# One early pair instead of three, and a different order of products, token transposes and gate rows in the feed-forward stage of a diffusion block

## Chip, cores and metric

The kernel runs on one core of a Trainium2 chip. The metric is the time of one execution on the device in microseconds; less is better. TensorE (PE) does the matmuls, ScalarE (ACT) and VectorE (DVE) move, split and combine tiles, and DMAs are issued from SyncE's queue (SP), from GpSimd's (POOL) and a few from ScalarE's.

## What is computed

One block of a bidirectional diffusion trunk on 640 tokens (128 of a prompt, 512 noisy ones) of width 1024: a mixer, then a feed-forward part with a gate. The change lies in the feed-forward part, whose reference is

```python
def block(x, cond, rows, states, w_ada, b_ada, norm1_w, norm2_w, mix_params, w_ff1, w_ff2):
    mod = (jax.nn.silu(cond) @ w_ada + b_ada)[:, None, :]
    sh1, sc1, g1, sh2, sc2, g2 = jnp.split(mod.astype(x.dtype), 6, axis=-1)
    ...
    x = x + g1 * y
    h = rmsnorm(x, norm2_w) * (1 + sc2) + sh2
    x = x + g2 * (jnp.square(jax.nn.relu(h @ w_ff1)) @ w_ff2)
    return x, new_states
```

w_ff1 is 1024 x 4096 and w_ff2 4096 x 1024. The conditioning differs between prompt and noisy tokens, so sc2, sh2 and g2 have two columns each.

## The kernel before

Every fp32 product is done as three matmuls of operands split into a high and a low part (`three`, lines 146 to 148: high by high, low by high, high by low). Splitting a tile is a copy on ScalarE (all ScalarE work has line 85) and a subtraction on DVE (line 107).

The 4096 hidden columns are 32 units of 128. Units 0 and 16 are done plainly (`plain`). Units p and p + 16 for p = 1 to 15 form a pair, whose 2 x 2 blocks are done with seven products instead of eight (`ff1`, `head`, `prod`): A11 and A12 into the PSUM tile pa, S2, S3 and A22 into pb, S1 and S4 into pc. The A's are halves of weights, the S's sums of them; the moving operands are input halves (hH, hL) and their sums T1 to T4 (tHL, and T4 in hH, hL). A product is 12 matmuls of 128x320 or 128x322. `ff2` then adds a pair's two hidden units into the output: ten sums of six matmuls 128x512, evacuated into y by ScalarE (the first pair's worth) or DVE (line 1278). One pair is 84 matmuls of the first kind and 60 of the second.

Weights come as follows. `direct` fetches A11 and A12 over POOL's queue: wh by a plain DMA (line 1147), its negative into wl by ScalarE, and the weight added into wl by an accumulating DMA (line 1149). `sums_of` loads s1 and s2 on SyncE's queue and forms S1 to S4 on DVE (lines 1029 to 1032). `second` loads the FF2 weights st2 on SyncE's queue and splits them. s1, s2 and st2 share a tag "st" with two buffers, s3 and gb a tag "sta" with two, wh and wl have three buffers each. SyncE's loads (`load`) keep the order of the program.

The order on each engine is made by a scheduler from the program and its priorities (`tc.high_priority()`), with `behind` for an order between two instructions of one engine that don't wait for each other by data. Every engine then runs its list in order.

`early(p)` does the products A11 and A12 ahead of the rest for p = 1, 2 and 3. Between these stand `to_tokens(0)` to `to_tokens(4)`: the 640 tokens of the residual are transposed back (40 transposes xT, line 1244), copied by ScalarE to xq and stored to DRAM as xtd over SyncE's queue (line 1246), to be added into y at pair 13. xq shares the tag "g" (four buffers) with the hidden units g. The vector cr, which `ada_dot` needs for the gate G2 at pairs 4 to 11, is read back from DRAM over SyncE's queue too (line 1236). At p = 12 `ada_bias` adds the bias and `g2_rows` turns G2's columns into rows: DVE spreads each of 16 columns over a 128x128 tile gb (line 1256), and PE transposes it (line 1257). m2 and m3 are the sums of products that DVE forms in sq (lines 1202 to 1205 and 1219); S3 goes into the same bank pb that m2 is read from, and A22 into the same bank that m3 is read from.

Of the kernel before, what the change touches and what calls it, by code (L numbers as in the profile page):

```python
# [19 lines left out]
P = 128  # L20
D = 1024
# [31 lines left out]
def hybrid_step(ctx: ExitStack, tc: tile.TileContext, I, O):  # L53
# [30 lines left out]
    def act(out, in_, func, **kw):  # L84
        ins = nc.scalar.activation(out, in_, func, **kw)  # L85
        if func in (AF.Exp, AF.Ln, AF.Silu, AF.Sigmoid):
            behind(ins.ins, tables["set"])
            tables["users"].append(ins.ins)
        return ins
# [925 lines left out]
    def comb(name):  # L1015
        return keep.tile([P, 4, HE], F32, tag="P%d" % (1 + int(name[1]) % 2), name=name)
# [2 lines left out]
        act(h, t_[:, :, 0:n], AF.Copy)  # L1019
        split_l(l, t_[:, :, 0:n], h)  # L1020

    def sums_of(p):
        s1 = stp.tile([P, 1024], F32, tag="st", name="s1")
        load(s1, I["wff1"][p])
        s2 = stp.tile([P, 1024], F32, tag="st", name="s2")
        load(s2, I["wff1"][p + 16])
        a, b = slice(0, 512), slice(512, 1024)
        s3 = stp.tile([P, 1024], F32, tag="sta", name="s3")[:, 0:512]
        tt(out=s3, in0=s1[:, a], in1=s2[:, a], op=ALU.subtract)  # L1029
        tt(out=s2[:, a], in0=s2[:, a], in1=s2[:, b], op=ALU.add)  # L1030
        tt(out=s1[:, a], in0=s2[:, a], in1=s1[:, a], op=ALU.subtract)
        tt(out=s1[:, b], in0=s1[:, b], in1=s1[:, a], op=ALU.subtract)
        return [("S1", s2[:, a]), ("S2", s1[:, a]), ("S3", s3)], (s2[:, b], s1[:, b])

    for b in range(4):
        def evac_o(acc):
            for f in range(2):
                k = 2 * b + f
                for hf, (lo, hi) in enumerate(SPANS):
                    for c, p0, p1 in pieces(lo, hi):  # L1040
                        stt(out=xr[:, k, p0:p1], in0=acc[f][hf][:, p0 - lo:p1 - lo], scalar=AB[:, G1, k, c:c + 1],
                            in1=xr[:, k, p0:p1], op0=ALU.mult, op1=ALU.add)
        proj_feat("wo", evac_o, part=o_part)
        for f in range(2):
            k = 2 * b + f
            square_add(sq2, xr[:, k, :], k, 0, T)
            for c, p0, p1 in CONDS:
                a2 = AB[:, SC2, k, c:c + 1]
                act(hH[:, k, p0:p1], xr[:, k, p0:p1], AF.Copy, scale=a2)
                stt(out=hL[:, k, p0:p1], in0=xr[:, k, p0:p1], scalar=a2, in1=hH[:, k, p0:p1].bitcast(F32),  # L1050
                    op0=ALU.mult, op1=ALU.subtract)
    r2 = ffp.tile([P, T], F32, name="r2")
    v2 = ffp.tile([P, T + 4], F32, name="v2")
    for lo, hi in SPANS:
# [9 lines left out]
    def unit(pool, name, src):  # L1064
        h = pool.tile([P, 512], F32R, tag=name + "h", name=name + "h")
        l = pool.tile([P, 512], F32R, tag=name + "l", name=name + "l")
        act(h, src, AF.Copy)
        split_l(l, src, h)
        return h, l

    def combined(p, out):
        with tc.high_priority():
            order_, rest = sums_of(p)
            for name, src in order_:
                out[name] = unit(sp, name, src)
        return rest

    def last_unit(out, src):
        with tc.high_priority():
            out["A22"] = unit(ff, "A22", src[0])  # L1080
            out["S4"] = unit(ff, "S4", src[1])

    splits = []

# [28 lines left out]
            act(hf[k // 4][:, :, T:T + 2], AB[:, SH2, k - 3:k + 1, :], AF.Copy)  # L1113
    zs = [plain(0)]
    ta, tb = comb("t1"), comb("t2")
    tt(out=ta[:, :, LO], in0=hf[0][:, :, HALF:T], in1=hf[0][:, :, LO], op=ALU.subtract)
    dve.tensor_copy(ta[:, :, HALF:HE], hf[0][:, :, T:T + 2])
    tt(out=tb, in0=hf[1][:, :, UP], in1=ta, op=ALU.subtract)
    store(tb, tH[:, 1], tL[:, 1])
    store(ta, tH[:, 0], tL[:, 0])  # L1120
    zs.append(plain(16))
    ta = comb("t3")
    tt(out=ta, in0=hf[1][:, :, UP], in1=hf[0][:, :, UP], op=ALU.subtract)
    store(ta, tH[:, 2], tL[:, 2])
# [49 lines left out]
            ins += three(ps[:, 0:n], A[0][:, s], A[1][:, s], B[0][:, k, :], B[1][:, k, :], start and k == 0, k == 3, skip=True)  # L1174
        return ins

    us = [v2[:, 0:HE], v2[:, HE:2 * HE], ff.tile([P, HE + 8], F32, name="u3")[:, 0:HE]]
    for t_ in us:
        dve.memset(t_[:, HALF:HE], 0.0)
    m2, m3 = sq2[:, 0:HE], sq2[:, HE:2 * HE]  # L1180
# [2 lines left out]
        return ff.tile([P, 2, T], F32R, tag="g", bufs=4, name="g")  # L1183

    def head(p, w):
        a = (xbank if p < 4 else bank)("pa")
        u = us[p % 3]
        prod(a, w["A11"], B11, True)
        act(u[:, LO], a[:, LO], AF.Copy)
        return a, u  # L1190

    def ff1(p, w, early=None):
        a, u = early or head(p, w)
        z0 = ffp.tile([P, T], F32, tag="u", bufs=2, name="z0")
        z1 = ffp.tile([P, T], F32, tag="u", bufs=2, name="z1")
        b = bank("pb")
        c = bank("pc")
        if early:
            tt(out=z0[:, LO], in0=a[:, LO], in1=r2[:, LO], op=ALU.mult)
        prod(b, w["S2"], T2, True)  # L1200
        prod(c, w["S1"], T1, True)
        tt(out=m2, in0=b[:, 0:HE], in1=u, op=ALU.add)
        prod(b, w["S3"], T3, False)
        tt(out=m3, in0=b[:, 0:HE], in1=u, op=ALU.add)
        tt(out=m3, in0=c[:, 0:HE], in1=m3, op=ALU.add)
        if not early:
            prod(a, w["A12"], B21, False)
            tt(out=z0[:, LO], in0=a[:, LO], in1=r2[:, LO], op=ALU.mult)
        ga, gb = g_tile(), g_tile()
        halves = ((HALF, T), (0, HALF)) if p == 15 else ((0, T),)  # L1210

        def z1_upper():
            tt(out=z1[:, HALF:T], in0=m3[:, LO], in1=r2[:, HALF:T], op=ALU.mult)

        if p == 15:
            z1_upper()
            finish(z1, m3[:, HALF:HE], gb, HALF)
        p3 = prod(c, w["S4"], B22, False)
        tt(out=m2, in0=c[:, 0:HE], in1=m2, op=ALU.add)
        tt(out=z0[:, HALF:T], in0=m2[:, LO], in1=r2[:, HALF:T], op=ALU.mult)  # L1220
        for lo, hi in halves:
            g0 = finish(z0, m2[:, HALF:HE], ga, lo, hi)
        p4 = prod(b, w["A22"], T4, False)
        if p == 15:
            behind(p4[0], p3[-1])
        if p < 15:
            z1_upper()
        tt(out=z1[:, LO], in0=b[:, LO], in1=u[:, LO], op=ALU.add)
        tt(out=z1[:, LO], in0=z1[:, LO], in1=r2[:, LO], op=ALU.mult)  # L1229
        g1 = finish(z1, m3[:, HALF:HE], gb, *halves[-1])  # L1230
        return g0, g1
# [1 line left out]
    cr = ff.tile([P, 2560], F32, tag="rows", name="cr")  # L1233
    junk = cr[:, 2048:2560].bitcast(BF16)
    cr = cr[:, 0:2048].rearrange("p (n k) -> p n k", k=D)
    nc.sync.dma_start(out=cr, in_=crd.unsqueeze(0).to_broadcast([P, 2, D]))
    xtd = dramp.tile([NT, P, D], F32, name="xtd")

    def to_tokens(c):
        t_ = ff.tile([P, 2, T], F32, tag="g", bufs=4, name="xq").rearrange("p i t -> p (i t)")  # L1240
        for q in range(2):
            pt = xbank("xT")
            for i in range(4):
                nc.tensor.transpose(pt[:, i * P:(i + 1) * P], xr[:, 4 * q + i, c * P:(c + 1) * P], ident)
            act(t_[:, 512 * q:512 * q + 512], pt, AF.Copy)
        nc.sync.dma_start(out=xtd[c], in_=t_[:, 0:D])

    def g2_rows():
        rows = ff.tile([P, 2, 1024], F32, tag="rows", name="g2r")
        for n in range(2):  # L1250
            for q in range(2):
                pt = xbank("g2")
                gb = stp.tile([P, 1024], F32, tag="sta", name="gb")
                for i in range(4):
                    s = slice(i * P, (i + 1) * P)
                    ts(out=gb[:, s], in0=ones, scalar1=AB[:, G2, 4 * q + i, n:n + 1], scalar2=None, op0=ALU.mult)
                    nc.tensor.transpose(pt[:, s], gb[:, s], ident)
                act(rows[:, n, 512 * q:512 * q + 512], pt, AF.Copy)
        return rows

# [41 lines left out]
            (nc.scalar if i else nc.sync).dma_start(out=O["out_y"][c, :, h], in_=y[:, c, h])  # L1302

    g = {0: tuple(finish(z, ub, g_tile()) for z, ub in zs)}
    heads, units = {}, {}

    def early(p):
        w = units.setdefault(p, {})
        w.update(direct(p))
        a, u = head(p, w)  # L1310
        prod(a, w["A12"], B21, False)
        heads[p] = (a, u)

    units[1] = {}
    last_unit(units[1], combined(1, units[1]))
    early(1)
    to_tokens(0)
    early(2)
    to_tokens(1)
    to_tokens(2)  # L1320
    early(3)
    to_tokens(3)
    to_tokens(4)
    y = ffp.tile([P, NT, D], F32, tag="X", name="y")
    for p in range(1, 16):
        w1 = units.get(p, {})
        if p > 1:
            last_unit(w1, combined(p, w1))
        if p > 3:
            w1.update(direct(p))  # L1330
        g[p] = ff1(p, w1, heads.get(p))
        if 4 <= p < 12:
            ada_dot(G2, p - 4, cr, junk, splits[-1])
        if p == 12:
            ada_bias(G2)
            rows = g2_rows()
        if p < 15:
            ff2(g.pop(p - 1), second(p - 1), acc_y(p - 1))
# [96 lines left out]
```

## Time and profile before

| | us |
|---|---|
| median of 3 runs | 840.62 |
| lowest, highest | 839.35, 843.19 |
| profiled execution | 841.95 |
| its span | 840.2 |
| PE busy in the span | 800.4 (95%) |
| DVE busy | 632.0 (75%) |
| ACT busy | 419.7 (50%) |
| POOL busy | 88.4 (11%) |

The span runs from the first to the last instruction of the profiled execution; 1.75 us of its time lie around it. Times in rows are counted from the span's start. The feed-forward stage begins at about 370 us. A matmul's row shows when it starts and how long it is in the pipeline; as matmuls overlap, what one costs is the distance between two starts. "xN" in a row joins N like instructions, and what stands in brackets is the idle time of the engine ahead of it and what ended that.

### The profile page before, as it was taken

Reading aid. Unit: us, or ns where it says so; the run is one execution under the profiler, and the core shown is the slowest. Engines: PE = TensorE matmul, PEld = TensorE weight load, DVE = VectorE, ACT = ScalarE, POOL = GpSimd, SP = SyncE. Lnnn points to the kernel's source line nnn. Section 1 sums busy time; section 2 is a strip of 40 time slices with the busy share of each in tenths; the row PEclk is TensorE's granted clock in tenths of the full one; section 3 lists DMA queues with packets and bytes.
Section 4 is the critical chain, followed back from the end, with each engine's and each line's share of the span. In section 5 each row is a group of like instructions: output and inputs, shape, how many; then the busy total and the mean of one; then the engine's idle time right before and its main releaser. Section 6 shows DMA issues by size and latency. Waiting matters only on the chain.

```text
span 840.2 us, 14783 instructions
## 1 busy us (share of the span) xinstructions
PE 800.4 (95%) x5842; PEld 705.6 (84%) x5842; DVE 632.0 (75%) x1188; ACT 419.7 (50%) x839; POOL 88.4 (11%) x123
## 2 busy tenths in 40 slices
PE   6999999999999999999899999999999998999995
PEld 2787688999988898998778898988899887788874
DVE  4668897868565569988467877787879878567858
ACT  5456458466554476655673444352345415324443
POOL 1121000030243003001000000000000000000200
PEclk9899999999999999999899999999999999899998
DMA  9926424141252073416642645545444535244923
GB/s 344 367 67 203 150 78 152 51 128 53 74 129 62 1 250 122 155 61 163 230 130 70 177 127 148 150 126 151 124 153 136 141 101 140 61 101 135 205 63 125
DMA packets 34197, 113.48 MB, mean 135 GB/s; under 512 B 4288, under 2 KB 5200, under 8 KB 33872
## 3 DMA queue, kind: packets, MB, share of 16 engines
q1 hardware_dynamic: 21888, 75.28, 26.5%
q0 software_dynamic: 8976, 30.50, 15.4%
q10 hardware_dynamic: 3264, 6.76, 2.3%
q8 instruction: 46, 0.75, 0.4%
q14 instruction: 23, 0.19, 0.1%
HBM read 106.66 MB, written 5.82 MB: 134 GB/s over the span
## 4 chain that ended last, share of the span: by engine, by line
PE 41%; issue 31%; DVE 12%; DMA 8%; ACT 5%; POOL 2%; DVEq 0%; SPq 0%; POOLq 0%; ACTq 0%
DMA st<-in_wff_dram 2%; PE ff L146 2%; PE ada L231 2%; PE ff L148 2%; PE ff L147 2%; PE pt L147 2%; PE pt L148 2%; PE pt L146 2%; DMA wh<-in_wff_dram 2%; PE pn L892 2%; PE pn L897 1%; DVE wl L107 1%; DMA xT<-in_xT_dram 1%; PE ob L148 1%; DMA s<-in_wff_dram 1%
## 5 line engine op out<-in xcount | busy, mean ns | idle before, releaser
L147 PE MATMUL ff<-wl,g 128*128 128x512 f32 x310 | 121.8, 396 | 0.0
L148 PE MATMUL ff<-wh,g 128*128 128x512 f32 x310 | 121.1, 396 | 0.0
L146 PE MATMUL ff<-wh,g 128*128 128x512 f32 x310 | 117.7, 399 | 3.3 <-ACT g L85 3.0
L1278 DVE TENSOR_TENSOR y<-ff,y 128x512 f32<-128x512 f32 x130 | 87.6, 688 | 10.7 <-PE ff L148 10.5
L107 DVE TENSOR_TENSOR wl<-st,wh 128x1024 fp32r<-128x1024 f32 x55 | 67.7, 1237 | 32.2 <-ACT wh L85 32.0
L85 ACT ACTIVATE wh<-st 128x1024 fp32r<-128x1024 f32 (+1 forms) x59 | 60.0, 1028 | 56.3 <-DMA st<-in_wff_dram 17.5
L146 PEld LDWEIGHTS ff<-wh,g 128*128 128x128 f32 x310 | 58.2, 189 | 16.3 <-ACT g L85 3.6
L148 PEld LDWEIGHTS ff<-wh,g 128*128 128x128 f32 x310 | 58.3, 188 | 13.4
L147 PEld LDWEIGHTS ff<-wl,g 128*128 128x128 f32 x310 | 58.5, 189 | 12.3
L147 PE MATMUL pt<-wl,hH 128*128 128x256 f32 x160 | 46.0, 288 | 0.2 <-DVE wl L107 0.2
L148 PE MATMUL pt<-wh,hL 128*128 128x256 f32 x160 | 45.6, 285 | 0.0
L146 PE MATMUL pt<-wh,hH 128*128 128x256 f32 x160 | 45.4, 286 | 0.0
L146 PE MATMUL pa<-hH,wh 128*128 128x320 f32 x120 | 38.8, 323 | 4.4 <-ACT u L85 3.7
L148 PE MATMUL pa<-hH,wl 128*128 128x320 f32 x120 | 38.8, 323 | 4.2 <-DMA wl<-in_wff_dram 4.2
L85 ACT ACTIVATE z<-z,sq 128x128 f32<-128x128 f32 (+3 forms) x62 | 31.4, 547 | 19.6 <-DVE z L1229 9.6
L85 ACT ACTIVATE S1h<-s 128x512 fp32r<-128x512 f32 x15 | 9.4, 628 | 62.7 <-DVE s L1030 45.9
L1147 POOL DMA_DIRECT2D wh<-in_wff_dram x15 | 8.4, 562 | 296.9 <-PE pa L148 197.7
L964 DVE SCALAR_TENSOR_TENSOR cr<-stg,cr 128x1024 f32<-128x1024 f32 (+1 forms) x32 | 39.1, 1220 | 0.1
L147 PE MATMUL pa<-hL,wh 128*128 128x320 f32 x120 | 38.3, 319 | 0.0
L1029 DVE TENSOR_TENSOR s<-s,s 128x512 f32<-128x512 f32 x15 | 10.4, 692 | 33.7 <-DMA s<-in_wff_dram 28.0
L107 DVE TENSOR_TENSOR g<-z,g 128x640 fp32r<-128x640 f32 (+1 forms) x34 | 25.9, 781 | 11.3 <-ACT g L85 11.3
L147 PEld LDWEIGHTS pt<-wl,hH 128*128 128x128 f32 x160 | 30.1, 188 | 3.3 <-issue 2.5
(459 smaller groups left out, 2414.4 us busy)
## 6 DMA issues: line engine op xcount, KB each, us to landing
st<-in_wff_dram SPq DMA_DIRECT2D x34, 512.0 KB, 3.7
sta<-in_ada_dram SPq DMA_DIRECT2D x32, 512.0 KB, 6.6
s<-in_wff_dram SPq DMA_DIRECT2D x30, 512.0 KB, 3.6
st<-in_win_dram SPq DMA_DIRECT2D x18, 512.0 KB, 3.7
stg<-in_adag_dram POOLq DMA_DIRECT2D x16, 512.0 KB, 3.8
wh<-in_wff_dram POOLq DMA_DIRECT2D x15, 512.0 KB, 3.9
wl<-in_wff_dram POOLq DMA_DIRECT2D x15, 512.0 KB, 5.5
st<-in_wout_dram SPq DMA_DIRECT2D x8, 512.0 KB, 3.9
```

The costliest lines, as they stand in the source:

```text
L85: ins = nc.scalar.activation(out, in_, func, **kw)
L107: return (eng or dve).tensor_tensor(out=dst, in0=src, in1=hi.bitcast(F32), op=ALU.subtract)
L146: first = mm(out, lhsT=ah, rhs=bh, start=start, stop=False, skip_group_check=skip)
L147: mm(out, lhsT=ah, rhs=bl, start=False, stop=False, skip_group_check=skip)
L148: return first.ins, mm(out, lhsT=al, rhs=bh, start=False, stop=stop, skip_group_check=skip).ins
L231: mm(pa[32 * i:32 * i + 32, 0:n], lhsT=sc[:, 4 * rnd + i, :], rhs=sts[i // m][:, n * (i % m):n * (i % m) + n], start=(rnd == 0), stop=(rnd ...
L892: mm(o[h2], lhsT=sbs[z][:, (2 * h2 + p) * P:(2 * h2 + p + 1) * P], rhs=vb[:, c, 2 * p + h2, :], start=True, stop=(c == 0))
L897: mm(o[h2], lhsT=qw[r, z, p, (c - 1) * P:c * P], rhs=C[j][r, 2 * z + p, :], start=False, stop=True)
L964: i = stt(out=junk, in0=st, scalar=1.0, in1=cr[:, n, :], op0=ALU.mult, op1=ALU.mult, accum_out=a)
L1029: tt(out=s3, in0=s1[:, a], in1=s2[:, a], op=ALU.subtract)
L1147: in_order(nc.gpsimd.dma_start(out=wh, in_=I["wff1"][p]))
L1278: tt(out=y[:, c, s], in0=ps, in1=y[:, c, s], op=ALU.add)
```

## The change

1. Only pair 1 is early. Its A11 and A12 are made from s1 by a copy and a subtraction, as the sums are, instead of two DMAs on POOL's queue, and its weights are called for right behind `plain(16)` at ordinary priority. All five `to_tokens` come behind its A11 and A12 in the program. Pairs 2 and 3 are done like the later ones.
2. In all other pairs A12 is the third product (S2, A12, S1, S3, S4, A22) where it was the fourth.
3. `g2_rows` gives PE one column of AB, repeated 128 times by a step of 0, as the operand to be transposed; gb and its 16 DVE instructions go.
4. u3 is 192 bytes longer, which moves all later tiles of its pool (g, A22, S4, rows) by as much.
5. The first sum t1 on DVE is ordered behind the last low part of the inputs.
6. The read of cr and the stores of xtd are issued on POOL's queue instead of SyncE's.

```diff
@@ sums_of
-    def sums_of(p):
+    def sums_of(p, out):
...
+        if p == 1:
+            wh = whp.tile([P, 1024], F32R, tag="wh", name="wh")
+            wl = wlp.tile([P, 1024], F32R, tag="wl", name="wl")
+            act(wh, s1, AF.Copy)
+            split_l(wl, s1, wh)
+            out["A11"], out["A12"] = (wh[:, a], wl[:, a]), (wh[:, b], wl[:, b])
...
-    tt(out=ta[:, :, LO], in0=hf[0][:, :, HALF:T], in1=hf[0][:, :, LO], op=ALU.subtract)
+    behind(tt(out=ta[:, :, LO], in0=hf[0][:, :, HALF:T], in1=hf[0][:, :, LO], op=ALU.subtract).ins, low.ins)
...
     zs.append(plain(16))
+    w1 = {}
+    s4 = combined(1, w1)
...
-    us = [v2[:, 0:HE], v2[:, HE:2 * HE], ff.tile([P, HE + 8], F32, name="u3")[:, 0:HE]]
+    us = [v2[:, 0:HE], v2[:, HE:2 * HE], ff.tile([P, HE + 56], F32, name="u3")[:, 0:HE]]
...
-        a = (xbank if p < 4 else bank)("pa")
+        a = (xbank if p < 2 else bank)("pa")
...
         prod(b, w["S2"], T2, True)
+        if not early:
+            prod(a, w["A12"], B21, False)
+            tt(out=z0[:, LO], in0=a[:, LO], in1=r2[:, LO], op=ALU.mult)
         prod(c, w["S1"], T1, True)
...
-        if not early:
-            prod(a, w["A12"], B21, False)
-            tt(out=z0[:, LO], in0=a[:, LO], in1=r2[:, LO], op=ALU.mult)
...
-    nc.sync.dma_start(out=cr, in_=crd.unsqueeze(0).to_broadcast([P, 2, D]))
+    nc.gpsimd.dma_start(out=cr, in_=crd.unsqueeze(0).to_broadcast([P, 2, D]))
...
-        nc.sync.dma_start(out=xtd[c], in_=t_[:, 0:D])
+        nc.gpsimd.dma_start(out=xtd[c], in_=t_[:, 0:D])
...
-                gb = stp.tile([P, 1024], F32, tag="sta", name="gb")
                 for i in range(4):
-                    s = slice(i * P, (i + 1) * P)
-                    ts(out=gb[:, s], in0=ones, scalar1=AB[:, G2, 4 * q + i, n:n + 1], scalar2=None, op0=ALU.mult)
-                    nc.tensor.transpose(pt[:, s], gb[:, s], ident)
+                    nc.tensor.transpose(pt[:, i * P:(i + 1) * P], AB[:, G2, 4 * q + i, n:n + 1].to_broadcast([P, P]), ident)
...
-    units[1] = {}
-    last_unit(units[1], combined(1, units[1]))
-    early(1)
-    to_tokens(0)
-    early(2)
-    to_tokens(1)
-    to_tokens(2)
-    early(3)
-    to_tokens(3)
-    to_tokens(4)
+    last_unit(w1, s4)
+    first = head(1, w1)
+    prod(first[0], w1["A12"], B21, False)
+    for c in range(NT):
+        to_tokens(c)
```

Three places show what this does to the engines' lists. First TensorE between the last matmuls ahead of FF2(0) and FF2(0) itself, before: S4 is the last product ahead of it, and head products of three pairs (pa, 72 matmuls) and all transposes stand further up.

```order
L146 MATMUL pc_4930<-hH_92,S4h_4759 128x322
L147 MATMUL pc_4930<-hL_93,S4h_4759 128x322
L148 MATMUL pc_4930<-hH_92,S4l_4760 128x322
L146 MATMUL ff2_5024<-wh_5014,g_4722 128x512
L146 MATMUL ff2_5032<-wh_5014,g_4722 128x512
L146 MATMUL ff2_5040<-wh_5014,g_4722 128x512
L147 MATMUL ff2_5024<-wl_5015,g_4722 128x512
```

In the kernel after the change, at the same place:

```order
L147 MATMUL pc_4867<-hL_93,S4h_4763 128x322
L148 MATMUL pc_4867<-hH_92,S4l_4764 128x322
L1250 MATMUL xT_4822<-kb_83,xr_3658 128x128 x4
L1250 MATMUL xT_4828<-kb_83,xr_3658 128x128 x4
L1250 MATMUL xT_4836<-kb_83,xr_3658 128x128 x4
L1250 MATMUL xT_4842<-kb_83,xr_3658 128x128 x4
L1250 MATMUL xT_4850<-kb_83,xr_3658 128x128 x4
L1250 MATMUL xT_4856<-kb_83,xr_3658 128x128 x4
L146 MATMUL pa_5075<-hH_92,wh_5070 128x320
L147 MATMUL pa_5075<-hL_93,wh_5070 128x320
L146 MATMUL ff2_4961<-wh_4951,g_4747 128x512
L147 MATMUL ff2_4961<-wl_4952,g_4747 128x512
```

Six sets of four transposes and two matmuls of pair 2's A11 now stand between S4 and FF2(0); 26 matmuls into pa stand ahead of FF2(0) instead of 72.

Second ScalarE ahead of FF2(0), before: the copies xq of the last two sets, the two splits wh of the FF2 weights st2, and the four bias-and-relu instructions and squares of pair 1's z.

```order
L85 ACTIVATE S4h_4759<-s1_4734 128x512
L85 ACTIVATE xq_4912<-xT_4913 128x512
L85 ACTIVATE xq_4912<-xT_4919 128x512
L85 ACTIVATE wh_5014<-st2_5012 128x1024
L85 ACTIVATE wh_5020<-st2_5018 128x1024
L85 ACTIVATE z1_4928<-z1_4928,sq2_3945 128x128
L85 ACTIVATE z1_4928<-z1_4928,sq2_3945 128x512
L85 ACTIVATE z0_4927<-z0_4927,sq2_3945 128x128
L85 ACTIVATE z0_4927<-z0_4927,sq2_3945 128x512
L85 ACTIVATE z1_4928<-z1_4928 128x640
L85 ACTIVATE y_4926<-ff2_5024 128x512
```

In the kernel after the change (the fifth copy is that of xT_4822):

```order
L85 ACTIVATE xq_4807<-xT_4814 128x512
L85 ACTIVATE wh_4951<-st2_4949 128x1024
L85 ACTIVATE z0_4864<-z0_4864,sq2_3945 128x128
L85 ACTIVATE z1_4865<-z1_4865,sq2_3945 128x128
L85 ACTIVATE z1_4865<-z1_4865,sq2_3945 128x512
L85 ACTIVATE z0_4864<-z0_4864,sq2_3945 128x512
L85 ACTIVATE wh_4957<-st2_4955 128x1024
L85 ACTIVATE z1_4865<-z1_4865 128x640
L85 ACTIVATE z0_4864<-z0_4864 128x640
L85 ACTIVATE xq_4821<-xT_4822 128x512
L85 ACTIVATE xq_4821<-xT_4828 128x512
L85 ACTIVATE xq_4835<-xT_4836 128x512
```

The first split of the FF2 weights has moved ahead of six copies xq; four z, the second split and two squares stand between the fourth and the fifth copy.

Third TensorE at pair 12, where the gate rows (g) are transposed, before. The first three rows are two matmuls of pair 13's A11 and the first of S4; S4's other matmuls are left out, and so are seven of the ten of A11 that follow the transposes.

```order
L146 MATMUL pa_7761<-hH_92,wh_7756 128x320
L147 MATMUL pa_7761<-hL_93,wh_7756 128x320
L146 MATMUL pc_7495<-hH_92,S4h_7469 128x322
...
L1257 MATMUL g2_7591<-kb_83,gb_7592 128x128 x4
L1257 MATMUL g2_7602<-kb_83,gb_7603 128x128 x4
L1257 MATMUL g2_7613<-kb_83,gb_7614 128x128
L148 MATMUL pa_7761<-hH_92,wl_7757 128x320
L146 MATMUL pa_7761<-hH_92,wh_7756 128x320
L147 MATMUL pa_7761<-hL_93,wh_7756 128x320
...
L1257 MATMUL g2_7613<-kb_83,gb_7614 128x128 x3
L1257 MATMUL g2_7624<-kb_83,gb_7625 128x128
L146 MATMUL ff2_7647<-wh_7637,g_7307 128x512
```

In the kernel after the change, with rows of S4 left out in the same way:

```order
L146 MATMUL pa_7740<-hH_92,wh_7735 128x320
L147 MATMUL pa_7740<-hL_93,wh_7735 128x320
L1260 MATMUL g2_7590<-kb_83,AB_94 128x128 x4
L1260 MATMUL g2_7596<-kb_83,AB_94 128x128 x4
L1260 MATMUL g2_7602<-kb_83,AB_94 128x128 x4
L146 MATMUL pc_7494<-hH_92,S4h_7468 128x322
...
L1260 MATMUL g2_7608<-kb_83,AB_94 128x128 x4
L146 MATMUL ff2_7626<-wh_7616,g_7306 128x512
L147 MATMUL ff2_7626<-wl_7617,g_7306 128x512
```

Twelve transposes have moved ahead of S4, and ten matmuls of A11, the first of which needs wl, have moved from behind the transposes to behind 30 matmuls of FF2.

## Rows read from the trace of the kernel before

**Rows 1.** Windows: stretch, length, busy PE, PEld, DVE, ACT, POOL, granted clock, DMA share, GB/s.
```profile
400.00:408.00 8.00, 5.85 (x26) 5.81 (x26) 4.11 (x7) 7.34 (x15) 0.52 (x1) 0.57 0.81 226
500.00:510.00 10.00, 10.00 (x53) 8.73 (x52) 8.22 (x15) 6.89 (x11) 0.89 (x1) 1.00 0.80 190
714.00:722.00 8.00, 5.84 (x20) 5.37 (x21) 1.52 (x3) 3.81 (x8) 0.00 (x0) 0.57 0.16 32
810.00:820.00 10.00, 9.33 (x40) 7.56 (x41) 6.46 (x13) 4.74 (x14) 0.00 (x0) 1.00 0.01 2
```

**Rows 2.** Timeline of PE, 390 to 441 us.
```profile
392.36 1.03 PE L1244 MATMUL xT<-kb,xr 128*128 128x128 f32 x8
...
402.15 0.63 PE L146 MATMUL pa<-hH,wh 128*128 128x320 f32 x1 [3.75 <-ACT u L85]
402.58 0.47 PE L147 MATMUL pa<-hL,wh 128*128 128x320 f32 x1
402.85 0.47 PE L148 MATMUL pa<-hH,wl 128*128 128x320 f32 x1
...
423.61 0.86 PE L146 MATMUL ff<-wh,g 128*128 128x512 f32 x3
...
425.71 0.86 PE L146 MATMUL ff<-wh,g 128*128 128x512 f32 x3
...
440.96 0.31 PE L148 MATMUL pb<-tHL,S2l 128*128 128x322 f32 x1
```

**Rows 3.** Timeline of SyncE's queue, 400 to 430 us.
```profile
404.97 11.25 SPq L1246 DMA_DIRECT2D xtd<-xq  x5
416.32 1.19 SPq L98 DMA_DIRECT2D st<-in_wff_dram  x2
```

**Rows 4.** Timeline of ACT, 420 to 428 us.
```profile
420.73 1.06 ACT L85 ACTIVATE wh<-st 128x1024 fp32r<-128x1024 f32 x1 [4.86 <-DMA st<-in_wff_dram]
...
425.02 1.93 ACT L85 ACTIVATE z<-z,sq 128x128 f32<-128x128 f32 x4 [2.00 <-DVE z L1229]
426.85 0.73 ACT L85 ACTIVATE z<-z 128x640 f32<-128x640 f32 x1
```

**Rows 5.** Timeline of DVE, 395 to 720 us.
```profile
395.34 0.15 DVE L1105 COPY ub<-ff 128x2 f32<-128x2 f32 x1
...
700.13 0.49 DVE L1202 TENSOR_TENSOR sq<-pb,v 128x322 f32<-128x322 f32 x1
...
719.87 0.69 DVE L1029 TENSOR_TENSOR s<-s,s 128x512 f32<-128x512 f32 x1 [5.73 <-PE g L1257]
```

**Rows 6.** Timeline of PE, 703 to 724 us.
```profile
703.41 0.31 PE L146 MATMUL pb<-tHL,S3h 128*128 128x322 f32 x1
...
705.04 0.31 PE L148 MATMUL pb<-tHL,S3l 128*128 128x322 f32 x1
...
709.00 0.42 PE L146 MATMUL pa<-hH,wh 128*128 128x320 f32 x1 [0.70 <-DMA wh<-in_wff_dram]
...
712.42 0.33 PE L1257 MATMUL g<-kb,gb 128*128 128x128 f32 x1 [0.20 <-DVE gb L1256]
716.16 0.64 PE L148 MATMUL pa<-hH,wl 128*128 128x320 f32 x1 [3.41 <-DMA wl<-in_wff_dram]
...
719.70 0.78 PE L146 MATMUL ff<-wh,g 128*128 128x512 f32 x1
...
723.46 0.38 PE L1257 MATMUL g<-kb,gb 128*128 128x128 f32 x2
```

**Rows 7.** Timeline of PE, 786 to 814 us.
```profile
792.70 1.43 PE L146 MATMUL ff<-wh,g 128*128 128x512 f32 x5 [1.07 <-ACT g L85]
...
810.67 0.51 PE L146 MATMUL ff<-wh,g 128*128 128x512 f32 x1 [1.98 <-ACT g L85]
```

**Rows 8.** The costliest groups of instructions: busy us, mean ns, idle before.
```profile
L107 DVE TENSOR_TENSOR wl<-st,wh 128x1024 fp32r<-128x1024 f32 x55 | 67.7, 1237 | 32.2 <-ACT wh L85 32.0
```

**Rows 9.** The chain that ended last, 700 to 820 us.
```profile
794.07 7.82 DMA st<-in_wff_dram
```

More of the change, by code (lines that the diff above doesn't have):

```diff
@@ L1049, in hybrid_step @@
                 act(hH[:, k, p0:p1], xr[:, k, p0:p1], AF.Copy, scale=a2)
-                stt(out=hL[:, k, p0:p1], in0=xr[:, k, p0:p1], scalar=a2, in1=hH[:, k, p0:p1].bitcast(F32),
-                    op0=ALU.mult, op1=ALU.subtract)
+                low = stt(out=hL[:, k, p0:p1], in0=xr[:, k, p0:p1], scalar=a2, in1=hH[:, k, p0:p1].bitcast(F32),
+                          op0=ALU.mult, op1=ALU.subtract)
     r2 = ffp.tile([P, T], F32, name="r2")
@@ L1071, in combined @@
     def combined(p, out):
[L1072 to L1075, printed above, removed]
+        order_, rest = sums_of(p, out)
+        for name, src in order_:
+            out[name] = unit(sp, name, src)
         return rest
     def last_unit(out, src):
-        with tc.high_priority():
-            out["A22"] = unit(ff, "A22", src[0])
-            out["S4"] = unit(ff, "S4", src[1])
+        out["A22"] = unit(ff, "A22", src[0])
+        out["S4"] = unit(ff, "S4", src[1])
     splits = []
@@ L1304, in hybrid_step @@
     g = {0: tuple(finish(z, ub, g_tile()) for z, ub in zs)}
[L1305 to L1312, printed above, removed]
-    units[1] = {}
-    last_unit(units[1], combined(1, units[1]))
-    early(1)
-    to_tokens(0)
-    early(2)
-    to_tokens(1)
-    to_tokens(2)
-    early(3)
-    to_tokens(3)
-    to_tokens(4)
+    last_unit(w1, s4)
[3 more added lines that the diff above has]
+        to_tokens(c)
     y = ffp.tile([P, NT, D], F32, tag="X", name="y")
     for p in range(1, 16):
-        w1 = units.get(p, {})
         if p > 1:
-            last_unit(w1, combined(p, w1))
-        if p > 3:
+            w1 = {}
+            with tc.high_priority():
+                last_unit(w1, combined(p, w1))
             w1.update(direct(p))
-        g[p] = ff1(p, w1, heads.get(p))
+        g[p] = ff1(p, w1, first if p == 1 else None)
         if 4 <= p < 12:
```

## The prediction

> **What bounds the kernel now.** I read first the windows of the feed-forward stage, then TensorE's timeline with its waits, then the queues of the engines that it waits for. In the steady middle TensorE is full: 10.00 of 10 us busy at a granted clock of 1.00 [rows 1]. There a matmul of 128x512 follows the last one after 0.234 us (423.61 to 425.71 for nine [rows 2]) and one of 128x322 after 0.148 us (703.41 to 705.04 for eleven steps [rows 6]). One pair takes 84 × 0.148 + 60 × 0.234 = 26.5 us whatever the order of its seven products, so an edit can only pay where TensorE stands still or runs at the half clock (1.2 instead of 2.4 GHz). From 390 us on there are three such places.
>
> Place A, the start of the pairs. At 402.15 TensorE has stood 3.75 us for the copy of u [rows 2]; the granted clock of 400 to 408 is then 0.57 [rows 1], and a 128x320 matmul takes 0.267 us (402.58 to 402.85 [rows 2]). The weights of the first second-layer sum are late too: SyncE's queue sits 11.25 us on the five stores of transposed tokens and issues the two loads only at 416.32 [rows 3]; ScalarE splits the first at 420.73 [rows 4], and FF2(0), the sum for units 0 and 16, begins at 423.61 [rows 2].
>
> Place C, pair 12. TensorE waits 0.70 us for wh, 0.20 for gb and 3.41 for wl [rows 6]; the clock of 714 to 722 is 0.57 [rows 1].
>
> Place D, the last pairs: 1.07 and 1.98 us, both for g [rows 7].
>
> **Place A, step by step.** Up to the first product of pair 1 (390.58) no engine's order that matters differs, so I start the walk there. DVE gets ahead of pair 1 what it did at 405 to 413 before: the split of A11/A12 (1.24 us [rows 8]), four sums and three low parts at about 0.6 each, since they follow each other faster than their 0.69 [rows 5], and m2 at 0.4: 5.8 us. Before, the bias ub was ready at 395.5 [rows 5]. Of the 5.8 us the low part of T4 (1.4) now comes behind ub, so ub is at 399.4 to 400. ScalarE then does four z (1.9 [rows 4]), one square and A22h (0.6 each, by the 0.73 of a square [rows 4] less the overlap) and DVE A22l (0.7, as the sum at 719.87 [rows 5]): about 403.2, where the second of the two "st" buffers is free and the first FF2 load can start.
>
> TensorE meanwhile: seven products, 84 × 0.148 = 12.4 us; 16 transposes, 0.1 each by the eight at 392.36 [rows 2], more where they come in fours: 2.1; small stalls for the low part of t3 (0.3) and for A22h, S4h and A22l (0.8 to 1.2). End of S4: 390.6 + 12.4 + 2.1 + 1.2 = 406.3. Then 24 transposes. The tenth set of four needs a PSUM buffer that ScalarE frees with the fifth copy xq, and that copy stands in ScalarE's queue behind the split of the first FF2 weights, four z, the second split and two squares (the order shown above). The load of 403.2 lands after the 4.4 us that this place took before (416.32 [rows 3] to 420.73 [rows 4]), at 407.6; then 1.06 + 1.93 + 1.06 + 2 × 0.7 [rows 4] and the copy itself: 413.3. TensorE has done the five sets by 408.8, so it stands **4.5 us**, more than the 3.75 before. As the clock fell after the 3.41 and the 3.75 us [rows 1, 2, 6], but not after the 1.98 at 810.67 (1.00 in 810 to 820 [rows 1, 7]), I let it fall again. Its price before was 12 × (0.267 − 0.148) = 1.4 us in head matmuls and up to 1 in the transposes; I take 1.9 for FF2 matmuls, between 1.5 and 2.5.
>
> FF2(0) begins at 414.2, 9.4 us earlier, but with only 26 of the 72 early head products done. To compare like with like: before, FF2(0) has ended at 440.96 [rows 2] with 72 head products and 14 matmuls of pair 2's S2 and S1 done. After, at the end of FF2(0) 36 head products are done, 50 fewer, which is 50 × 0.148 = 7.4 us: the equal point of before is 433.6. After: 414.2 + 60 × 0.234 + 10 × 0.148 + 1.9 = 431.6. **Gain 2.0 us**: three wasted stretches become one long one. Bounds: no half clock and a stall of 3.6, gain 4 to 5; loads that land late (below), loss 1.4; more stalls in pair 2, loss 3.
>
> **Stores and the broadcast on POOL's queue.** What the row shows is a wait and not a transfer: the 11.25 us on SyncE [rows 3] end with the last copy xq. Taking the five stores out of that queue lets the loads start when their buffer is free; that is in the 414.2. On POOL's queue wh of pair 2 is issued between the stores, behind the second copy xq (407), and must land by 414 (411.5 with the 4.4 us of a load); wl of pair 2 is issued behind the fourth store, at about 416, and is first used at about 423. Both fit; if wl takes 7.8 us as a load did in the tail [rows 9], 1 us is lost.
>
> The Trainium skill, "DMA: Bandwidth & Descriptors", section "Issuing engines are not separate DMA queues", says that transfers started by different engines run on the same 16 DMA engines and that a second issuer saves sequencer time only. By it the saving would be the wait at the head of SyncE's queue and nothing of the transfers; the row agrees as far as it goes, and the rival below takes the rest of the rule as a mechanism.
>
> **Place C.** g2_rows no longer needs DVE's 16 multiplications. Most of them were hidden, since DVE stood 5.73 us behind the last one [rows 5]; on the path they cost the 0.20 us. What counts is the order: ten head products stood behind gb and the first of them waited for wl until 716.16 [rows 6]. Now the transposes stand before S4 and 30 FF2 matmuls follow; the first use of wl comes at about 720 (709.0 + 0.3 for two head matmuls + 1.4 for 12 transposes + 1.8 for S4 + 0.4 for the last four + 30 × 0.234), 4 us after it landed. What goes: 3.41 + 0.20 us of waits; 10 × 0.119 = 1.2 for head matmuls at half clock; 12 FF2 matmuls took 3.76 instead of 2.81 (719.70 to 723.46 [rows 6]), 0.95; slow transposes and the pipeline's refilling, 0.4. **Gain 6.2 us.** The 0.70 for wh stays, as does a wait of 0.9 for m3 ahead of it. A stationary operand of step 0 does not occur in the trace: between nothing and each transpose taking twice its 0.1 us [rows 2], 1.6 us. I take nothing: the operand is loaded in the place where gb was loaded, 128 columns of it as before.
>
> **Place D.** Before pair 14's sum g's high part now stands in front of a weight split in ScalarE's queue, so I let the 1.07 go, with 0.1 of refilling: **gain 1.2 us**. The 1.98 stays.
>
> **At nothing.** A12 third: the steady middle has no gap to fill (10.00 of 10 [rows 1]), and S3 must still follow m2. Pair 12 of before shows the same order already: m2 at 700.13 [rows 5], S3 at 703.41 without a wait [rows 6]. The shift of g by 192 bytes: the spacing of 0.234 holds for all of FF2 and that of 0.148 for stationary tiles on either side of u3, so place is not seen to matter. Against the 0.213 us that 512 columns take at 2.4 GHz there are 20 ns that it could touch, on some 930 matmuls; I keep −5 and +9 us as far ends. The order of the first sum behind the last low part moves one DVE operation while TensorE still has the plain units to do, until 390.6.
>
> **Sum.** −2.0 − 6.2 − 1.2 = −9.4 us. Against the profiled execution (841.95) that is 832.6, against the median, which is 1.3 lower, 831.2. I say **832.0 us**, between the two.
>
> **Rivals.**
> - *The stall at A is short.* If ScalarE gets z before the first FF2 weights land, the fifth xq comes by 411 and the clock stays. For it: z of S4 is ready at 408. Against: both splits still stand ahead. Gain 2.5 to 4 us more: 828.5.
> - *Loads share the engines.* The two FF2 loads start beside the broadcast of 1 MB and pair 2's wh. In the tail such a load took 7.82 us [rows 9], 3.4 more than the 4.4 at this place; that gives 835.4 to 836. Against: the 4.4 were measured in the same stretch.
> - *Place C's wait moves.* DVE's s3 sum stands ahead of m3 of pair 12 and of G2's bias; if pair 13's loads land late, A22 and the transposes wait instead. Given back 5 to 6: 837 to 838.
> - *Slower, by m2.* S3 now comes right behind A12 in several pairs, with no FF2 between; m2 has the 24 × 0.148 = 3.6 us of S1 and A12. If DVE's queue brings it late, TensorE stands in each of the 11 plain pairs. From 0.85 us a pair (m2 3.8 us later than at pair 12) the gain is gone; at 1.3 us it is 845. Against: m2 began 0.2 us after S2's end at pair 12.
> - *It does nothing.* Not possible at C: the wait for wl is gone by order alone.
>
> **How the numbers follow.** Forecast 0.5 (829.5 to 834.5); short stall 0.2; shared engines 0.14; moved wait 0.1; m2 0.06. A measurement of this kernel tells 0.5% (4.2 us) from nothing: faster is below 836.4. Faster: 0.5 + 0.2 + 0.13 + 0.02 = 0.85; same 0.01 + 0.08 + 0.01 = 0.10; slower, from m2 alone, 0.05. The range 826 to 838 leaves out m2, the far ends of g and a little of either side.
>
> **What the profile of after would show.** A: no wait for u at 402; one wait of 3.5 to 6 us on a transpose xT, for xq, at about 409 to 413; FF2(0) from 414; one halved stretch behind it. C: no wait of pa for wl, clock 1.00 from 710 to 730. D: one wait for g instead of two. Middle: spacings 0.234 and 0.148 as now. I'm wrong if the middle shows new waits of pb for m2, if a 128x512 matmul's spacing moves by more than 3 ns, or if A holds two waits.

## The result and the profile after

The changed kernel takes 828.6 us (median of 4 runs, 827.78 to 832.44) against 839.99 (4 runs, 839.34 to 843.19); the ratio is 0.9866 with a 95% interval of 0.9825 to 0.9907. Its profiled execution, the fastest of the four, took 827.78 us with a span of 826.0.

The windows of the kernel after, in the columns of [rows 1]:

```profile
410.00:420.00 10.00, 5.20 (x20) 4.50 (x21) 3.65 (x4) 8.25 (x15) 1.98 (x3) 0.66 0.95 340
...
500.00:510.00 10.00, 10.00 (x50) 8.55 (x49) 9.22 (x17) 7.61 (x12) 0.00 (x0) 1.00 0.51 167
...
700.00:710.00 10.00, 8.81 (x58) 7.96 (x57) 9.19 (x21) 5.63 (x11) 0.88 (x1) 1.00 0.56 138
710.00:720.00 10.00, 10.00 (x46) 8.26 (x45) 7.39 (x12) 4.50 (x8) 0.00 (x0) 1.00 0.36 117
```

The middle is as full as before. At pair 12, now at 700 to 720, the clock stays at 1.00, where it was 0.57 in 714 to 722 [rows 1]. At the start of the pairs one bad stretch has moved to 410 to 420: 5.20 of 10 us busy at 0.66.

TensorE's timeline of the kernel after:

```profile
390.18 0.31 PE L146 MATMUL pa<-hH,wh 128*128 128x320 f32 x1
...
402.34 0.42 PE L146 MATMUL pb<-hH,A22h 128*128 128x320 f32 x1 [1.06 <-ACT A22h L85]
...
414.80 1.12 PE L1250 MATMUL xT<-kb,xr 128*128 128x128 f32 x4 [6.23 <-ACT xq L85]
...
416.25 0.63 PE L146 MATMUL ff<-wh,g 128*128 128x512 f32 x1
...
417.53 0.45 PE L146 MATMUL ff<-wh,g 128*128 128x512 f32 x1
...
432.09 0.31 PE L146 MATMUL pb<-tHL,S2h 128*128 128x322 f32 x1
...
702.02 0.41 PE L146 MATMUL pb<-hH,A22h 128*128 128x320 f32 x1 [0.95 <-DVE sq L1213]
...
704.30 0.42 PE L146 MATMUL pa<-hH,wh 128*128 128x320 f32 x1 [0.23 <-DMA wh<-in_wff_dram]
...
710.99 0.39 PE L146 MATMUL ff<-wh,g 128*128 128x512 f32 x1
...
711.44 0.39 PE L148 MATMUL ff<-wh,g 128*128 128x512 f32 x1
...
713.48 0.39 PE L148 MATMUL ff<-wh,g 128*128 128x512 f32 x1
...
796.58 0.50 PE L146 MATMUL ff<-wh,g 128*128 128x512 f32 x1 [1.48 <-ACT g L85]
```

The wait for u [rows 2], the wait for wl [rows 6] and the 1.07 us for g [rows 7] are gone. In their place stands one wait of 6.23 us on the tenth set of transposes, and ahead of it one of 1.06 us for A22h, which the prediction had among its small stalls. Behind the long wait matmuls are slow until 417.53: two of 128x320 and three of 128x512 (0.43 us apart). FF2(0) begins at 416.25 where it began at 423.61 [rows 2].

The chain of work that ended last, around that wait:

```profile
403.04 6.14 DMA st<-in_wff_dram
...
410.17 1.90 ACT z L85 x4
...
413.55 0.72 ACT z L85
414.27 0.49 ACT xq L85
```

The load of FF2's first weights started at 403.04, where the walk had put it (403.2), but landed 6.14 us later, not 4.4; ScalarE's splits, biases and squares follow as listed, and the fifth copy xq at 414.27 ends the wait.

One thing in the timeline is not a wait. Two of its rows, at 711.44 and 713.48, are FF2 matmuls nine apart. That is 2.04 us for nine, 0.227 us each; before it was 0.234 [rows 2]. Over the feed-forward stage the mean distance of neighbouring 128x512 matmuls (some 900 pairs of starts under 0.26 us apart) is 228.0 ns against 233.4.

For the experiments I also give the length of the feed-forward stage in the profiled execution, from pair 1's first product to TensorE's last matmul (or transpose): 439.6 us before, 425.4 after. It leaves out the part of the program ahead of it, whose length varies by some 2 us between executions without any change in it.

### The profile page after: what moved, and what is told of

Read it like the earlier page. It is cut to its first block, busy times and chain, and to the rows that moved or that the text cites. A ratio compares the mean times of both kernels' runs of the same rounds, so it can differ in the third digit from the quotient of the medians.

```text
span 826.0 us, 14769 instructions
## 1 busy us (share of the span) xinstructions
PE 790.1 (96%) x5842; PEld 702.9 (85%) x5842; DVE 628.9 (76%) x1173; ACT 417.5 (51%) x839; POOL 89.9 (11%) x127
## 4 chain that ended last, share of the span: by engine, by line
PE 64%; DVE 13%; issue 13%; DMA 4%; ACT 4%; POOL 1%; DVEq 0%; SPq 0%; POOLq 0%; ACTq 0%
PE ff L146 6%; PE ff L148 6%; PE ff L147 6%; PE ada L231 2%; PE pt L147 2%; PE pt L148 2%; PE pt L146 2%; PE pn L892 2%; PE pb L148 2%; PE pb L146 2%; PE pb L147 2%; PE pn L897 1%; DMA st<-in_wff_dram 1%; DVE wl L107 1%; DMA s<-in_wff_dram 1%
## 5 line engine op out<-in xcount | busy, mean ns | idle before, releaser
L85 ACT ACTIVATE S4h<-s 128x512 fp32r<-128x512 f32 x15 | 9.5, 631 | 50.9 <-PE pc L147 50.9
```

## The experiments

The experiments ran in three sets, each together with the kernel before; a ratio is to the kernel before of its own set. Where a run is compared with the changed kernel, two ratios are subtracted, and some 4 us either way of such a difference are noise. The lists of the engines and the places of the tiles are those of the built programs.

**g back in its old place.** Of the change, only the length of u3 is undone.

```diff
-    ... ff.tile([P, HE + 56], F32, name="u3")[:, 0:HE]]
+    ... ff.tile([P, HE + 8], F32, name="u3")[:, 0:HE]]
```

> The changed kernel with u3 at its old length, so that g, A22, S4 and the rows lie 192 bytes lower, as before; no engine's order differs. Theory place: the 128x512 matmuls of FF2, 0.234 us apart before and 0.228 after, go back to 0.234 in every pair, and with some 930 of them the time rises by about 5 us to 833.5. Rival company: the spacing fell because other engines and DMAs run differently beside them; then it stays 0.228 and the time 828.6.

Measured: 832.38 us, 0.9915 (0.9894 to 0.9936); stage 429.7. TensorE's timeline, nine FF2 matmuls apart:

```profile
440.46 0.39 PE L148 MATMUL ff<-wh,g 128*128 128x512 f32 x1
...
442.56 0.39 PE L148 MATMUL ff<-wh,g 128*128 128x512 f32 x1
```

2.10 us, 0.233 each; the mean of the stage is 233.3 ns. All engines run the same lists in both kernels, so company falls and place stands. By the ratios the place is worth 0.0049 × 840 = 4.1 us; by the spacing 930 × 5.3 ns = 4.9.

**The shift alone, in the kernel before.**

```diff
-    ... ff.tile([P, HE + 8], F32, name="u3")[:, 0:HE]]
+    ... ff.tile([P, HE + 56], F32, name="u3")[:, 0:HE]]
```

> The kernel before with only u3 lengthened by 192 bytes; no engine's order differs. Theory place: spacing 0.228, time 840.0 - 5.1 = 834.9. Rival company: 0.234 and 840.0.

Measured: 836.24 us, 0.9945 (0.9925 to 0.9966), 4.6 us faster; spacing 227.9 ns. Place again.

**All tiles shifted, in the kernel before.**

```diff
-    cb = const.tile([P, CB_W], F32, name="cb")
+    pad, cb = const.tile([P, 48], F32, name="pad"), const.tile([P, CB_W], F32, name="cb")
```

> The kernel before with one pad of 192 bytes ahead of everything, so that g lies where it lies in the changed kernel (160 bytes behind a multiple of 512) but wh and wl have moved with it (352). Theory place, absolute: g's own address counts, so 0.228 and 834.9. Theory place, relative: what counts is that g and the moving wh and wl lie alike within 512 bytes, so 0.234 and 840.0.

Measured: 840.73 us, 1.0012 (0.9996 to 1.0028); spacing 233.5 ns. g lies exactly as in the changed kernel and nothing is gained, so g's own address does not decide. What g must fit is something that moved with it here; the other SBUF operands of these matmuls are wh and wl, which stream while g is loaded as the stationary operand. The simplest reading is that the distance between the two counts. That the place of each counts by itself, g's and that of wh and wl both best at 160, is not excluded: no run puts both at a new place with distance 0.

**Three other places of g.** In the changed kernel u3 has HE + 16, HE + 24 and HE + 40 elements. Each was executed once.

> The changed kernel with u3 lengthened so that g begins at a multiple of 512 bytes (wh and wl at 160, so 352 behind them within 512). Theory equal place: only the same place within 512 bytes helps; spacing 0.233, about 833. Rival aligned start: g at a round address is as good or better; 0.228 or less.

> The same with g at 32 (384 behind wh within 512, a multiple of 128). Theory equal place: 0.233, about 833. Rival period: the places need only agree within 128 bytes; then 0.228.

> The same with g at 96 (448 behind wh within 512, a multiple of 64 but not of 128). Theory equal place: 0.233, about 833. Rival period: agreement within 64 bytes is enough, 0.228; before, at 480, the distance was 320, a multiple of 64 as well, and gave 0.233.

| g, bytes behind a multiple of 512 | wh, wl | distance within 512 | spacing, ns | kernel |
|---|---|---|---|---|
| 160 | 160 | 0 | 228.0 | after |
| 96 | 160 | 64 | 229.8 | after, HE + 40 |
| 32 | 160 | 128 | 232.4 | after, HE + 24 |
| 0 | 160 | 160 | 233.7 | after, HE + 16 |
| 480 | 160 | 192 | 233.4 | before |
| 160 | 352 | 192 | 233.5 | before, all shifted |

(The distance is taken the shorter way round. In all rows wh and wl lie behind g by it; the other side was not run, and that 512 bytes are the period is assumed, not tested.) Neither rival holds: a round address is no better than the old place, and agreement within 64 or 128 bytes isn't enough. Nor is it all or nothing, as "equal place" had it: the spacing grows with the distance up to about 160 bytes. The times of the single executions were 830.48 (g at 96), 833.2 (at 32) and 835.91 us (at 0).

**The new g2_rows alone, in the kernel before.**

```diff
-                gb = stp.tile([P, 1024], F32, tag="sta", name="gb")
...
-                    ts(out=gb[:, s], in0=ones, scalar1=AB[:, G2, 4 * q + i, n:n + 1], scalar2=None, op0=ALU.mult)
-                    nc.tensor.transpose(pt[:, s], gb[:, s], ident)
+                    nc.tensor.transpose(pt[:, i * P:(i + 1) * P], AB[:, G2, 4 * q + i, n:n + 1].to_broadcast([P, P]), ident)
```

> The kernel before with only the new g2_rows. Theory order: with gb gone the scheduler puts twelve transposes ahead of S4 and the ten A11 matmuls behind 30 matmuls of FF2, the 3.41 us wait for wl and the slow clock go, 840.0 - 6.2 = 833.8. Rival moved wait: A22, m3 or the loads of pair 13 wait instead, 838 to 840.

Measured: 831.25 us, 0.9904 (0.9879 to 0.9930), 8.1 us faster; stage 430.8. TensorE's waits from 370 us on (total, times, longest):

```profile
PE pa L146 <- ACT u L85: 3.5, 1, 3.5
...
PE ff L146 <- ACT g L85: 1.5, 1, 1.5
...
PE pa L148 <- DMA wl<-in_wff_dram: 0.8, 1, 0.8
```

The 3.41 us for wl are gone (the 0.8 is that of 395), and of the two waits for g only one is left, shorter. So this edit carries place C and place D as well: DVE and ScalarE reach the last pairs with other lists. The stage is 8.8 us shorter than before.

**The old g2_rows in the changed kernel** (the same diff, reversed).

> The changed kernel with the old g2_rows (16 DVE multiplications into gb). Theory order: the transposes go back behind S4, ten A11 matmuls stand ahead of FF2 and wait for wl, the clock halves; 828.6 + 6 = 834.6. Rival: the early pairs and the queues have changed what pair 12 waits for, and it costs under 1 us.

Measured: 833.69 us, 0.9933 (0.9910 to 0.9956), 5.6 us slower than the changed kernel's ratio; stage 432.4, 7.0 longer. Its waits:

```profile
PE xT L1250 <- ACT xq L85: 6.3, 1, 6.3
PE pa L148 <- DMA wl<-in_wff_dram: 3.0, 1, 3.0
PE ff L146 <- ACT g L85: 1.5, 1, 1.5
```

The wait for wl is back with 3.0 us, and so is the order of before: nine transposes, ten A11 matmuls, then FF2. The order at pair 12 is the cause, whatever the start of the pairs looks like. Place D does not come back: there is one wait for g, of 1.5 us, as in the changed kernel. So the new g2_rows is enough to remove the other one, but not needed for it.

**The stores and the broadcast back on SyncE's queue.**

```diff
-    nc.gpsimd.dma_start(out=cr, in_=crd.unsqueeze(0).to_broadcast([P, 2, D]))
+    nc.sync.dma_start(out=cr, in_=crd.unsqueeze(0).to_broadcast([P, 2, D]))
...
-        nc.gpsimd.dma_start(out=xtd[c], in_=t_[:, 0:D])
+        nc.sync.dma_start(out=xtd[c], in_=t_[:, 0:D])
```

> The changed kernel with the broadcast of cr and the five stores xtd back on SyncE's queue. All five stores then stand ahead of the two loads of FF2's weights there. Theory queue: the loads are issued only when the last copy xq is stored, at about 416 instead of 403, and land at about 420; FF2(0) begins at about 423 instead of 416; with head products of pair 2 filling part of it, 4 to 7 us slower, 833 to 836. Rival transfers: the same 16 DMA engines carry all of it anyway, so moving the issue is worth under 1 us: 828 to 829.5.

Measured: 833.21 us, 0.9929 (0.9909 to 0.9950), 5.3 us slower than the changed kernel's ratio. SyncE's queue:

```profile
403.11 8.83 SPq L1252 DMA_DIRECT2D xtd<-xq  x5
412.05 1.20 SPq L98 DMA_DIRECT2D st<-in_wff_dram  x2
```

And TensorE:

```profile
407.34 0.66 PE L1250 MATMUL xT<-kb,xr 128*128 128x128 f32 x4 [1.33 <-ACT xq L85]
417.58 2.50 PE L146 MATMUL ff<-wh,g 128*128 128x512 f32 x5 [9.58 <-ACT wh L85]
```

All five stores hold the queue for 8.83 us, the loads start at 412.05 instead of 403.04, and TensorE waits 9.58 us for the split of FF2's weights. The stage is 432.2 us, 6.8 longer. Pair 1's first product starts 2.57 us earlier in this execution (387.61 against 390.18); counted from it, FF2(0) begins at 29.97 us instead of 26.07. The queue theory holds in place and size, though FF2(0) comes at 417.58 and not at 423: for the rest, the copies xq, no longer behind the splits in ScalarE's list, were done earlier than I had it. The Trainium skill, "DMA: Bandwidth & Descriptors", section "Issuing engines are not separate DMA queues", grants a second issuer only the sequencer's time. The measurement agrees that the transfer is not made faster: the load took some 4.4 us here (412.05 to the split at 416.47) and 6.14 in the changed kernel. What the edit saves is the 8.83 us for which the queue stood behind stores that waited for their data.

**A12 fourth again, in the changed kernel.**

```diff
         prod(b, w["S2"], T2, True)
-        if not early:
-            prod(a, w["A12"], B21, False)
-            tt(out=z0[:, LO], in0=a[:, LO], in1=r2[:, LO], op=ALU.mult)
...
         tt(out=m3, in0=c[:, 0:HE], in1=m3, op=ALU.add)
+        if not early:
+            prod(a, w["A12"], B21, False)
+            tt(out=z0[:, LO], in0=a[:, LO], in1=r2[:, LO], op=ALU.mult)
```

> The changed kernel with A12 the fourth product again (S2, S1, S3, A12). Theory nothing: the steady middle is full, so 828.6 within 1 us. Rival: A12 third gives DVE the time for m2 and removes waits of S3; without it small waits on pb come back in the eleven plain pairs, 2 to 4 us.

Measured: 827.43 us, 0.9868 (0.9840 to 0.9895), the changed kernel's ratio. No wait of S3 comes back. By the times A12's place is worth nothing that can be measured; the lower end of the rival's 2 to 4 us is not excluded by them. The profiled execution is the slowest of the four, 830.2 us, and its stage is 427.6, 2.2 longer than in the changed kernel. Most of the difference lies in the last pair:

```profile
791.62 0.41 PE L146 MATMUL pc<-hH,S4h 128*128 128x322 f32 x1 [1.30 <-DVE sq L1211]
...
797.41 0.50 PE L146 MATMUL ff<-wh,g 128*128 128x512 f32 x1 [1.98 <-ACT g L85]
...
798.28 0.63 PE L147 MATMUL ff<-wl,g 128*128 128x512 f32 x1
798.71 0.63 PE L146 MATMUL ff<-wh,g 128*128 128x512 f32 x1
```

In the last pair S4 waits 1.30 us for m3, which it does not do in the changed kernel, and behind the wait for g, 1.98 us instead of 1.48, seven FF2 matmuls run at the half clock (granted 0.50 in 798.3 to 801.2). The kernel before had the same wait of 1.98 us, and the clock stayed at 1.00 [rows 1, 7].

**What is left of the change without place A.** The kernel before with the longer u3 and the new g2_rows.

> The kernel before with the longer u3 and the new g2_rows together, but with its three early pairs, A12 fourth and the stores on SyncE's queue. What it lacks against the changed kernel is place A. Theory gain: place A is worth the 2.0 us that the prediction gave it, so this is 830.6. Rival nothing: the long wait for xq gives back all that the shorter list saves, so this is as fast as the changed kernel, 828 to 829, or up to 2 us faster by the sum of the two runs alone (840 - 4.5 - 8.8 = 826.7).

Measured: 826.24 us, 0.9837 (0.9814 to 0.9860); stage 425.0 against 425.4. The gain theory falls: one early pair, A12 third, the queues and the order on DVE together add nothing that can be measured to these two edits; the intervals overlap, and the middle of this one lies 2.4 us on the faster side.

**Both splits first.** In the changed kernel ScalarE does both splits of FF2(0)'s weights directly behind the fourth copy xq, then the copies of the third token block, then pair 1's bias and relu.

```diff
-                act(wh, st, AF.Copy)
+                i = act(wh, st, AF.Copy).ins
+                if p == 0:
+                    for z_ in relus:
+                        behind(z_, i)
+                    if f:
+                        behind(copies[4], i)
+                        for z_ in relus:
+                            behind(z_, copies[5])
```

> The changed kernel with ScalarE's list at the start of the pairs ordered by hand: both splits of FF2's first weights directly behind the fourth copy xq, then the copies of the third token block, then pair 1's bias, relu and squares. Theory list: the wait of the tenth set of transposes (6.2 us) ends with the fifth copy, which now comes about 3.5 us earlier (411.7 instead of 414.7), and FF2(0) begins at about 412.7 instead of 416.2; 825 to 826, and 824 if the clock no longer falls. Rival: the late load (6.1 us) sets it, or pair 1's g comes late for FF2(1) and the wait moves there; 828 to 829.

Measured: 825.14 us, 0.9833 (0.9808 to 0.9857), the fastest median of all; the ratio is 2.8 us better than the changed kernel's, with overlapping intervals, and the stage 424.0, 1.4 shorter. ScalarE's timeline:

```profile
408.94 1.06 ACT L85 ACTIVATE wh<-st 128x1024 fp32r<-128x1024 f32 x1 [3.15 <-DMA st<-in_wff_dram]
410.16 1.06 ACT L85 ACTIVATE wh<-st 128x1024 fp32r<-128x1024 f32 x1 [0.16 <-DMA st<-in_wff_dram]
411.52 1.09 ACT L85 ACTIVATE xq<-xT 128x512 f32<-128x512 f32 x2 [0.31 <-DMA xtd<-xq]
412.49 1.91 ACT L85 ACTIVATE z<-z,sq 128x128 f32<-128x128 f32 x4
```

And TensorE's:

```profile
412.17 1.11 PE L1261 MATMUL xT<-kb,xr 128*128 128x128 f32 x4 [4.44 <-ACT xq L85]
412.94 0.78 PE L146 MATMUL ff<-wh,g 128*128 128x512 f32 x1
```

The wait is 4.44 instead of 6.23 us and FF2(0) begins at 412.94, as the list theory said (0.8 us of the difference to 416.25 is an earlier start of pair 1). The fifth copy no longer waits for the biases; it now waits for the two splits and, 0.31 us, for the store that frees its buffer. The clock still falls, for five FF2 matmuls.

## Why the prediction was right, and where it was wrong

The time (832.0 forecast, 828.6 measured) lay in the range, and faster was the likeliest case. The sum of 9.4 us was made of terms that were partly wrong and partly set each other off. That the total fits is in part luck: with g in its old place, which is what the sum was worked out for, the kernel takes 832.38, because place A gave less than its term and places C and D more; and the largest miss, the place of g, happened to fit into the range.

- **Place C was right** and a little small. From wh's first product to the twelfth FF2 matmul's end it was 14.46 us before (709.00 to 723.46 [rows 6]) and is 6.69 after (704.30 to 710.99). Ten head matmuls fewer and three transposes more lie in it (1.5 − 0.3), so 6.6 us are gone, and 0.47 of the wait for wh, which the forecast left as it was: 7.1 against 6.2. The wait for wl is gone by order, so the change does what it says; the rival that moves the wait did not occur: m3's wait ahead of A22 is 0.95 us, against the 0.9 of the forecast.
- **Place D was right**: one wait for g, not two, 1.48 us. What brings it about was not named: the new g2_rows alone does, and the rest of the change does without it. Its price of 1.2 us leaves out the clock: the forecast let it stay behind the wait of 1.98 us, as in the trace of before, but behind waits of 1.98 to 2.00 us it fell for seven FF2 matmuls, some 1.4 us, in the profiles of A12 fourth, all tiles shifted and g at 0. The trace of before shows one of two outcomes.
- **Place A was mis-sized.** The wait came where it was forecast, for the reason that was forecast, but with 6.23 us for 4.5, since the load took 6.14 us for 4.4: the second rival, shared engines, in half its size. The run with the stores and the broadcast back on SyncE's queue bears it out: there the broadcast and the stores are issued ahead of the load, and it took some 4.4 us again; in the 6.14 us the DMA engines moved some 2.0 MB, in the 4.38 us of before some 1.3 MB, at nearly the same rate (323 and 305 GB/s). The clock fell, but came back after five slow matmuls, about 1 us and not 1.9. The equal point of before is 433.6 − 390.6 = 43.0 us behind the first head product; after, the end of FF2(0) and ten head products lies at 432.09 − 390.18 = 41.9. Of the 1.1 us some 0.3 are FF2's shorter spacing, so place A gave 0.7 of the forecast 2.0 in this execution, and nothing measurable against the run that has only the longer u3 and the new g2_rows.
- **"Place is not seen to matter" was the step that failed.** The forecast took the shift of g at nothing, with −5 us as a far end. That end is what happened: 5.4 ns on some 930 matmuls, 5.0 us, and a spacing moved by more than 3 ns is one of the prediction's own signs of being wrong. The evidence that I read was no evidence: the 128x320 matmuls whose stationary operand lay on either side of u3 stream hH and tHL, which lie at many distances. Was there a clue in the rows? At the half clock (1.2 GHz) a matmul of 320 columns took 0.267 us [rows 2] and one of 512 took 0.427 (416.25 to 417.53 for three), one column a period; half of that, 0.133 and 0.213 us, is an estimate of the columns' own time at 2.4 GHz. By it 0.148 is 15 ns over and 0.234 is 20 ns over, and the shift took just these 5 ns away. But the trace of before has, from 300 us on, mean spacings of 117.5 ns for back-to-back matmuls of 256 columns and 174 to 175 for those of 384, 11 and 14 to 15 ns over, so a remainder that grows with the columns would have looked ordinary. Only moving g tells.
- **A12 third and m2** were right at nothing for the steady middle, where no wait of pb for m2 came; in the last pair A12's place moved a wait (above), within the noise of the times.

So 5.0 (place of g), 7.1 (C), 1.7 (D, with the half us by which the second wait is shorter) and 0.7 (A) make 14.5, against 14.2 us by which the stage is shorter. This is the account of two executions, 841.95 and 827.78 us: the one of before lies 2.0 us above its median and the one of after is the fastest of its four. By the medians 11.4 us are gained. The single undoings by ratio are smaller too, 4.1 us for the place and 5.6 for g2_rows (whose undoing leaves place D as it is), each with some 4 us of noise either way.

## What to carry to other kernels

Where long rows of 128x512 matmuls follow each other without a gap, try another distance of the stationary operand from the moving one: a pad of 192 bytes is a cheap edit, and here it was worth 4 to 5 us. A forecast that takes such a shift at nothing needs a row in which the same matmuls lie at two distances. When an instruction behind a slow load stands in an engine's list, look at everything behind it: here TensorE waited 6.23 us for a copy because a split whose load was under way stood ahead of it. An edit that removes work from an engine with idle time can still pay, because the scheduler makes another order.

## What the runs showed of the hardware

The spacing of back-to-back 128x512 matmuls of FF2 changes with the place of the stationary operand against the moving one within 512 bytes: 228.0 ns at distance 0, 229.8 at 64 bytes, 232.4 at 128, 233.4 to 233.7 at 160 and 192. The stationary operand's own address does not decide it (228.0 and 233.5 with g at 160). For the matmuls 128x320 and 128x322 no such gain is seen: their mean spacing was 148.2 ns in the kernel before and 148.5 with the shift alone, which moves A22 and S4 too; over the many distances that occur among them in eight of the kernels, the means lie between 145 and 152 ns without a trend. The Trainium skill, "SBUF — State Buffer", section "Who interferes with whom", gives TensorE two read ports, one for the moving operand and one for the weights, and calls them independent. From that alone one would expect no effect of the place; measured are up to 5.7 ns a matmul, and the measurement decides. Why the place counts, no run here shows.
